# A GpSimd product written in output order, a subtraction moved behind background work, and down blocks with 512 columns

## The chip, the cores and the metric

The kernel runs on one core of a Trainium2 chip. The metric is the device time of one execution in microseconds (us), the lower the better. The core has five engines that run side by side, each with its own in-order queue: PE (TensorE, the matmuls, with the weight loads shown as PEld), DVE (VectorE), ACT (ScalarE), POOL (GpSimd) and SP (SyncE, which here starts the DMAs). They wait for each other through semaphores.

## What is computed

The reference is a block of two attention kinds (MoBA and differential) with an expert layer (PEER), followed by two more attention layers, all in fp32 on 256 tokens of width 1024. The change touches the expert layer alone:

```python
def chunk_fn(xc):                      # tokens of 1024 features
    q = (xc @ w_query).reshape(C, PEER_HEADS, 2, PEER_HALF)
    sc = jnp.einsum('thpd,hpnd->thpn', q, sub_keys)
    top_s, top_i = lax.top_k(sc, PEER_TOPK)
    ...                                # best 16 of the pairs: experts, best_s
    gates = jax.nn.softmax(best_s, axis=-1)
    u = expert_down[experts]
    vv = expert_up[experts]
    act = gelu(jnp.einsum('cd,chkd->chk', xc, u), approximate=False)
    w = gates * act
    return jnp.einsum('chk,chkd->cd', w, vv)
```

There are 16384 experts (128 x 128), 8 heads and 16 chosen experts per head and token.

## The kernel before

**Tiling of the expert layer.** No expert is gathered. The kernel multiplies all tokens with all 16384 down vectors, in 128 blocks of 128 experts, takes the Gelu, multiplies with a dense matrix of gates G (nearly all zero), and multiplies the result with all up vectors, again in 128 blocks. Experts lie on the partitions, the 256 tokens on the free axis. The tile `big` has 100 slots of 128 x 256 for the blocks between down and up; down blocks 100 to 127 use slots 0 to 27 again, so the order (`seq`, in `peer`) is: down 0 to 99, up 0 to 15, down 100 to 115, up 16 to 27, down 116 to 127, up 28 to 127. Blocks go in pairs: `d_pair(j)` makes down blocks j and j+1, `u_pair(j)` up blocks j and j+1.

**fp32 by three products.** Every fp32 operand is split into a hi part (rounded to fp32r) and a lo part (the rest), and `mm3` (L217 to L221) does hi x hi, hi x lo, lo x hi as three matmuls into one PSUM accumulation. Weights arrive as raw fp32 by DMA; `Stream` (L76 to L152) splits each unit of 1024 columns into wh (ACT cast, L119) and wl (DVE subtraction, L129), three units ahead of use. The tokens' parts are nh and nl. A down block is 8 steps of k with three matmuls of 256 columns each. An up block takes the activations as weights: `w_split(j)` makes gh (ACT cast, L892) and gl (DVE subtraction, L893) of a pair's `big` slots one block ahead, and `sum_unit` runs 4 x 3 matmuls of 512 columns.

**Ticks.** G comes in 64 ticks of four tokens for each half of the experts, as background work: `later` queues a step, `run_bg(budget)` after each block runs some two of them. `g_tick` (L913 to L943) makes one-hots o1 and o2 of the two expert indices on DVE (L921, L922), o1h = o1 x gate on GpSimd (L923, written through a rearranged view, so with a step of 64 elements for each new token), and o1l = o1 x lo part of the gate by four ACT activations (L926). Two ticks later `mm` runs the eight small matmuls of the tick (L934, L935) into a bank of PSUM; every second tick DVE multiplies the finished G into `big` (L941). The first half's ticks run beside down blocks 64 to 99, the second half's beside up blocks 28 to 61.

**Queues.** Everything is in program order on each engine. In an up block the order is: `stream.get` (casts of later weights), the 12 matmuls, for the first block of a pair `w_split` of the next pair (gh, then gl), then `run_bg` (the ticks). PSUM has two banks with tag s; a down pair takes one bank for both blocks, and its Gelu (L881) reads the whole bank after the second block.

Of the kernel before, what the change touches and what calls it, by code (L numbers as in the profile page):

```python
# [10 lines left out]
F32R = mybir.dt.float32r  # L11
# [3 lines left out]
AF = mybir.ActivationFunctionType  # L15
ALU = mybir.AluOpType
AX = mybir.AxisListType

P = 128
# [135 lines left out]
class Kernel:  # L155
# [614 lines left out]
    def peer(self, x):  # L770
        tc, nc, A = self.tc, self.nc, self.A
        ident = self.const("ident")
        SLOTS, H = 100, 64
        with (
# [1 line left out]
            tc.tile_pool(name="pew", bufs=3) as pw,  # L776
        ):
            big = pl.tile([P, SLOTS, 256], F32, name="big")
            nh = pl.tile([P, 8, 256], F32R, name="nh")
            nl = pl.tile([P, 8, 256], F32R, name="nl")  # L780
            qT = big[:, 64:80, :]
            sc = big[:, 80:96, :].rearrange("p (t a) b -> p t (a b)", t=2).rearrange("p t (h n) -> p t h n", n=P)
            sk = big[:, 56:64, :].rearrange("p a b -> p (a b)")
# [5 lines left out]
            ghT = pl.tile([P, 256], F16, name="ghT")  # L789
# [16 lines left out]
            TB, GB = 1.5, 1.75  # L806
            with tc.tile_pool(name="peq", bufs=1) as pq:
# [32 lines left out]
                for hp in range(16):  # L840
                    if hp % 2 == 0:
                        qb = self.bank("s")
                    wh, wl = self.stream.get(self.u, hp > 0)
                    o = qb[:, (hp % 2) * 256 : (hp % 2) * 256 + 256]
                    for k in range(8):
                        ks = slice(k * P, k * P + P)
# [20 lines left out]
            with tc.tile_pool(name="pew2", bufs=2) as pw2:  # L867
                def d_pair(j, nxt, budget):
                    hb = self.bank("s")
                    for jj in range(2):  # L870
                        wh, wl = self.stream.get(self.u)
                        if jj == 0 and nxt is not None:
                            w_split(nxt)
                        o = hb[:, jj * 256 : jj * 256 + 256]
                        for k in range(8):
                            ks = slice(k * P, k * P + P)
                            self.mm3(o, wh[:, ks], wl[:, ks], nh[:, k, :], nl[:, k, :], k == 0, k == 7)
                        self.u += 1
                        if jj:
                            sl = j % SLOTS  # L880
                            nc.scalar.activation(  # L881
                                big[:, sl : sl + 2, :].rearrange("p a b -> p (a b)"), hb, AF.Gelu
                            )
                        self.run_bg(budget)

                Ws = {}

                def w_split(j):
                    sl = j % SLOTS
                    wh = pw2.tile([P, 2, 256], F32R, name=self.nm("gh"), tag="gh")  # L890
                    wl = pw2.tile([P, 2, 256], F32R, name=self.nm("gl"), tag="gl")
                    nc.scalar.copy(wh, big[:, sl : sl + 2, :])  # L892
                    nc.vector.tensor_sub(wl, big[:, sl : sl + 2, :], wh)  # L893
                    Ws[j] = (wh, wl)

                def u_pair(j, nxt, budget):
                    if j not in Ws:
                        w_split(j)
                    gh, gl = Ws.pop(j)
                    for jj in range(2):  # L900
                        self.sum_unit(
                            lambda t: (gh[:, jj, t * P : t * P + P], gl[:, jj, t * P : t * P + P]),
                            banks,
                            j + jj == 0,
                            x if j + jj == 127 else None,
                        )
                        if jj == 0 and nxt is not None:
                            w_split(nxt)
                        self.run_bg(budget)

                gp = {}

                def g_tick(half, tb):  # L913
                    def f():
                        tsl = slice(tb * 4, tb * 4 + 4)
                        o2 = pw2.tile([P, P, 4], F16, name=self.nm("o2"), tag="o2", bufs=3)
                        o1 = pw2.tile([P, H, 4], F16, name=self.nm("o1"), tag="o1", bufs=3)
                        o1h = pw2.tile([P, 4, H], F16, name=self.nm("o1h"), tag="o1h", bufs=3)
                        o1l = pw2.tile([P, 4, H], F16, name=self.nm("o1l"), tag="o1l", bufs=3)
                        b = lambda a, n: a[:, tsl].unsqueeze(1).to_broadcast([P, n, 4])  # L920
                        nc.vector.tensor_tensor(o1, iota4[:, half * H : half * H + H, :], b(i1T, H), op=ALU.is_equal)  # L921
                        nc.vector.tensor_tensor(o2, iota4, b(i2T, P), op=ALU.is_equal)  # L922
                        nc.gpsimd.tensor_tensor(o1h.rearrange("p t j -> p j t"), o1, b(ghT, H), op=ALU.mult)  # L923
                        for i in range(4):
                            t = tb * 4 + i
                            nc.scalar.activation(o1l[:, i, :], o1[:, :, i], AF.Copy, scale=glT[:, t : t + 1])  # L926

                        def mm():
                            if tb % 2 == 0:
                                gp[0] = self.bank("t" if tb % 4 == 0 else "o")  # L930
                            g = gp[0]
                            for i in range(4):
                                o = g[:, ((tb % 2) * 4 + i) * H : ((tb % 2) * 4 + i) * H + H]
                                nc.tensor.matmul(o, o2[:, :, i], o1h[:, i, :], start=True, stop=False)  # L934
                                nc.tensor.matmul(o, o2[:, :, i], o1l[:, i, :], start=False, stop=True)  # L935
                            if tb % 2:
                                t8 = slice(tb // 2 * 8, tb // 2 * 8 + 8)
                                gv = g.rearrange("p (t j) -> p j t", t=8)
                                for j0, j1, s0 in ((0, 64, 0),) if half == 0 else ((0, SLOTS - 64, 64), (SLOTS - 64, 64, 0)):
                                    v = big[:, s0 : s0 + j1 - j0, t8]  # L940
                                    nc.vector.scalar_tensor_tensor(v, gv[:, j0:j1, :], 2.0**-14, v, op0=ALU.mult, op1=ALU.mult)  # L941

                        return mm  # L943

                    return f

                def g_ticks(half):
                    pend = []
                    LAG = 2

                    def step(tb):
                        def f():
                            if tb < 64:
                                pend.append(g_tick(half, tb)())
                            if tb >= LAG:
                                pend.pop(0)()

                        return f

                    for tb in range(64 + LAG):  # L960
                        self.later(step(tb), 0, 0.89)

                self.scores(3, qT, sk, sc, rx, top)
                self.later(lambda: self.select(pw, topv, topi, i1T, i2T, ghT, glT, big), 0, 0.5)
                M = 128 - SLOTS
                seq = [("D", j) for j in range(0, SLOTS, 2)]
                for u0, u1 in ((0, 16), (16, M)):
                    seq += [("U", j) for j in range(u0, u1, 2)]
                    seq += [("D", j) for j in range(SLOTS + u0, SLOTS + u1, 2)]
                seq += [("U", j) for j in range(M, 128, 2)]  # L970
                for i, (kind, j) in enumerate(seq):
                    if (kind, j) == ("D", 64):
                        self.flush()
                        g_ticks(0)
                    if (kind, j) in (("D", SLOTS - 2), ("U", 62)):
                        self.flush()
                    if (kind, j) == ("U", 0):
                        banks = [self.bank(f"a{i}") for i in (1, 3, 2, 0)]
                    if (kind, j) == ("U", M):
                        g_ticks(1)  # L980
                    nxt = None
                    if i + 1 < len(seq) and seq[i + 1][0] == "U":
                        nxt = seq[i + 1][1]
                    if kind == "D":
                        d_pair(j, nxt, TB if j < 64 else GB)
                    else:
                        u_pair(j, nxt, GB)

# [771 lines left out]
```

## Time and profile before

| what | value |
|---|---|
| median of 3 runs | 1459.81 us (1459.66 to 1462.8) |
| profiled execution | 1459.06 us |
| its span, first to last instruction | 1457.3 us |
| granted TensorE clock, mean | 0.996 of 2.4 GHz |
| PE busy | 1420.3 us, 97% of the span |
| DVE, ACT, POOL busy | 991.8, 884.2, 409.0 us |

The span is a little shorter than the execution's time, and the profiled execution is 0.75 us below the median of the runs. Matmuls are pipelined: a record of 0.28 us can be followed by the next start 0.12 us later, so the cadence is read from starts, not from durations. DVE and ACT records overlap their successor by some 0.08 us. Blocks stand in time as follows: down 0 to 99 from 197 to 506 us, up 0 to 15 to 549 us, down 100 to 115 to 596 us, up 16 to 27 to 628 us, down 116 to 127 to 663 us, up 28 to 127 to 979 us.

### The profile page before, as it was taken

What the parts mean: (1) busy time and instruction counts of PE and PEld (TensorE: products, weight loads), DVE (VectorE), ACT (ScalarE), POOL (GpSimd) and SP (SyncE); (2) the same over time, 40 slices, a digit from 0 to 9 for tenths busy, and PEclk for the clock granted to TensorE, in tenths of its full rate; (3) what the DMA queues carried; (4) which work ended last, traced back from release to release, by engine and by line L of the source; (5) the groups of instructions that cost most, each with busy time, mean ns of one, the idle gap of its engine ahead of it and who ended that gap; (6) DMA issues with size and microseconds to landing.
All of it is one profiled execution on the core that took longest, in us unless ns stands there. A gap on an engine that the chain in (4) does not pass through costs nothing.

```text
span 1457.3 us, 24829 instructions
## 1 busy us (share of the span) xinstructions
PE 1420.3 (97%) x9375; PEld 1240.1 (85%) x9375; DVE 991.8 (68%) x1985; ACT 884.2 (61%) x1723; POOL 409.0 (28%) x626
## 2 busy tenths in 40 slices
PE   9899999999999999999888999999999999999998
PEld 7677999999999989897666888887888888887887
DVE  6666899997699854548999555556554566665444
ACT  5675554544699844547878454456766667766653
POOL 4760300000377500004666000007232543117200
PEclk9999999999999999999999999999999999999999
DMA  7334445555444455554333555565444554445422
GB/s 252 142 116 150 150 172 190 184 178 182 165 146 148 172 202 175 196 180 144 123 139 118 201 201 198 183 225 172 164 173 157 172 188 157 148 164 194 168 97 87
DMA packets 50935, 243.14 MB, mean 167 GB/s; under 512 B 4224, under 2 KB 11520, under 8 KB 31488
## 3 DMA queue, kind: packets, MB, share of 16 engines
q1 hardware_dynamic: 50528, 241.04, 47.3%
q8 instruction: 73, 1.20, 0.3%
q10 hardware_dynamic: 288, 0.52, 0.1%
q14 instruction: 46, 0.38, 0.1%
HBM read 240.50 MB, written 1.05 MB: 166 GB/s over the span
## 4 chain that ended last, share of the span: by engine, by line
PE 82%; DVE 5%; POOL 5%; ACT 5%; issue 3%; DMA 1%; DVEq 0%; ACTq 0%; POOLq 0%
PE a L219 14%; PE a L221 14%; PE a L220 14%; PE s L219 10%; PE s L220 10%; PE s L221 9%; PE s L1365 2%; DVE big L941 1%; ACT wh L119 1%; ACT o1l L926 1%; DVE o L921 1%; DVE o L922 1%; PE o L1441 1%; PE o L1449 1%; DVE wl L129 1%
## 5 line engine op out<-in xcount | busy, mean ns | idle before, releaser
L129 DVE TENSOR_TENSOR wl<-raw,wh 128x1024 fp32r<-128x1024 f32 (+1 forms) x435 | 565.3, 1308 | 140.3 <-ACT wh L119 140.3
L119 ACT CAST wh<-raw 128x1024 fp32r<-128x1024 f32 (+1 forms) x435 | 452.7, 1043 | 258.4 <-PE a L221 187.5
L923 POOL TENSOR_TENSOR o1h<-o,ghT 128x256 f16<-128x256 f16 x128 | 170.7, 1453 | 468.2 <-DVE o L921 456.0
L219 PE MATMUL s<-nh,wh 128*128 128x256 f32 x1024 | 292.6, 286 | 0.0
L220 PE MATMUL s<-nl,wh 128*128 128x256 f32 x1024 | 289.7, 283 | 0.0
L221 PE MATMUL s<-nh,wl 128*128 128x256 f32 x1024 | 289.6, 283 | 0.0
L219 PE MATMUL a<-wh,gh 128*128 128x512 f32 x512 | 202.7, 396 | 0.0
L221 PE MATMUL a<-wh,gl 128*128 128x512 f32 x512 | 199.7, 390 | 0.0
L220 PE MATMUL a<-wl,gh 128*128 128x512 f32 x512 | 199.2, 389 | 0.0
L219 PEld LDWEIGHTS s<-nh,wh 128*128 128x128 f32 x1024 | 196.5, 192 | 0.1
L220 PEld LDWEIGHTS s<-nl,wh 128*128 128x128 f32 x1024 | 196.5, 192 | 0.1
L221 PEld LDWEIGHTS s<-nh,wl 128*128 128x128 f32 x1024 | 196.3, 192 | 0.0
L926 ACT ACTIVATE o1l<-o,glT 128x64 f16<-128x64 f16 x512 | 138.1, 342 | 32.3 <-DVE o L921 25.7
L219 PE MATMUL a<-wh,xha 128*128 128x512 f32 x320 | 132.4, 414 | 0.5 <-DVE xha L282 0.5
L221 PE MATMUL a<-wh,xla 128*128 128x512 f32 x320 | 125.4, 392 | 0.0
L220 PE MATMUL a<-wl,xha 128*128 128x512 f32 x320 | 125.2, 391 | 0.0
L893 DVE TENSOR_TENSOR gl<-big,gh 128x512 fp32r<-128x512 f32 x64 | 44.3, 692 | 106.9 <-ACT gh L892 106.9
L221 PEld LDWEIGHTS a<-wh,gl 128*128 128x128 f32 x512 | 96.1, 188 | 20.8
L220 PEld LDWEIGHTS a<-wl,gh 128*128 128x128 f32 x512 | 96.3, 188 | 18.9
L219 PEld LDWEIGHTS a<-wh,gh 128*128 128x128 f32 x512 | 96.3, 188 | 18.8
L881 ACT ACTIVATE big<-s 128x512 f32<-128x512 f32 x64 | 38.1, 595 | 91.6 <-PE s L221 91.4
L1370 DVE CUSTOM_DVE_ANT_0 e<-s,bias 128x128 f32<-128x128 f32 (+2 forms) x128 | 34.1, 327 | 71.2 <-PE s L1365 71.2
(409 smaller groups left out, 2499.5 us busy)
## 6 DMA issues: line engine op xcount, KB each, us to landing
raw<-in_peer_down_dram SPq DMA_DIRECT2D x64, 1024.0 KB, 4.8
raw<-in_peer_up_dram SPq DMA_DIRECT2D x64, 1024.0 KB, 4.9
raw<-in_a_w_in_dram SPq DMA_DIRECT2D x40, 1024.0 KB, 4.9
raw<-in_b_w_in_dram SPq DMA_DIRECT2D x16, 1024.0 KB, 4.8
raw<-in_w_in_dram SPq DMA_DIRECT2D x10, 1024.0 KB, 5.0
raw<-in_peer_query_dram SPq DMA_DIRECT2D x8, 1024.0 KB, 4.8
raw<-in_w_out_dram SPq DMA_DIRECT2D x4, 1024.0 KB, 5.0
bias<-in_bias_dram SPq DMA_DIRECT2D x8, 512.0 KB, 5.8
```

What stands on the lines that cost most here:

```text
L119: self.nc.scalar.copy(hi[:, c], self.part(u)[:, c])
L129: eng.tensor_sub(lo[:, c], self.part(u)[:, c], hi[:, c])
L219: nc.tensor.matmul(o, lh, rh, start=start, stop=False)
L220: nc.tensor.matmul(o, lh, rl, start=False, stop=False)
L221: nc.tensor.matmul(o, ll, rh, start=False, stop=stop)
L881: nc.scalar.activation(big[:, sl : sl + 2, :].rearrange("p a b -> p (a b)"), hb, AF.Gelu)
L893: nc.vector.tensor_sub(wl, big[:, sl : sl + 2, :], wh)
L921: nc.vector.tensor_tensor(o1, iota4[:, half * H : half * H + H, :], b(i1T, H), op=ALU.is_equal)
L923: nc.gpsimd.tensor_tensor(o1h.rearrange("p t j -> p j t"), o1, b(ghT, H), op=ALU.mult)
L926: nc.scalar.activation(o1l[:, i, :], o1[:, :, i], AF.Copy, scale=glT[:, t : t + 1])
L1365: nc.tensor.matmul(o, l, r, start=start, stop=stop)
L1370: nc.vector.tensor_tensor_reduce(e[:, c], s[:, c], bts[i][:, qt * w : qt * w + w], -1.0, 3.0e38, ALU.add, ALU.min, nmx[g][:, h, qt : qt + 1],)
```

## The change

Three edits, all in `peer`.

nh and nl become two halves of one tile nhl, so that for each k the 256 columns of nh and the 256 of nl lie side by side. A new `d_dual` takes down pairs 50 to 62 and 100 to 126; in it wh meets both parts in one matmul of 512 columns, wl meets nh in one of 256, each block has a bank of its own, ACT copies the half that came from nl out of PSUM, DVE adds the other half to it, and the Gelu runs once per pair from `big`. `w_split` does its cast at once and returns the subtraction as a function; down pairs call it at once, `u_pair` after `run_bg`. The product o1h is written in the order of its tile, and o1 is read through a rearranged view instead.

```diff
-            nh = pl.tile([P, 8, 256], F32R, name="nh")
-            nl = pl.tile([P, 8, 256], F32R, name="nl")
+            nhl = pl.tile([P, 8, 2, 256], F32R, name="nhl")
+            nh, nl = nhl[:, :, 0, :], nhl[:, :, 1, :]
...
                         if jj == 0 and nxt is not None:
-                            w_split(nxt)
+                            w_split(nxt)()
...
+                def d_dual(j, nxt, budget):
+                    sl = j % SLOTS
+                    for jj in range(2):
+                        hb = self.bank("s")
+                        wh, wl = self.stream.get(self.u)
+                        if jj == 0 and nxt is not None:
+                            w_split(nxt)()
+                        for k in range(8):
+                            ks = slice(k * P, k * P + P)
+                            nc.tensor.matmul(hb, wh[:, ks], nhl[:, k, :, :].rearrange("p a b -> p (a b)"), start=k == 0, stop=False)
+                            nc.tensor.matmul(hb[:, 0:256], wl[:, ks], nh[:, k, :], start=False, stop=k == 7)
+                        self.u += 1
+                        v = big[:, sl + jj, :]
+                        nc.scalar.copy(v, hb[:, 256:512])
+                        nc.vector.tensor_tensor(v, hb[:, 0:256], v, op=ALU.add)
+                        if jj:
+                            v = big[:, sl : sl + 2, :].rearrange("p a b -> p (a b)")
+                            nc.scalar.activation(v, v, AF.Gelu)
+                        self.run_bg(budget)
...
                     nc.scalar.copy(wh, big[:, sl : sl + 2, :])
-                    nc.vector.tensor_sub(wl, big[:, sl : sl + 2, :], wh)
                     Ws[j] = (wh, wl)
+                    return lambda: nc.vector.tensor_sub(wl, big[:, sl : sl + 2, :], wh)
...
-                        if jj == 0 and nxt is not None:
-                            w_split(nxt)
+                        low = w_split(nxt) if jj == 0 and nxt is not None else lambda: None
                         self.run_bg(budget)
+                        low()
...
-                        nc.gpsimd.tensor_tensor(o1h.rearrange("p t j -> p j t"), o1, b(ghT, H), op=ALU.mult)
+                        nc.gpsimd.tensor_tensor(o1h, o1.rearrange("p j t -> p t j"), ghT[:, tsl].unsqueeze(2).to_broadcast([P, 4, H]), op=ALU.mult)
...
                     if kind == "D":
-                        d_pair(j, nxt, TB if j < 64 else GB)
+                        (d_dual if j >= SLOTS or 50 <= j < 64 else d_pair)(j, nxt, TB if j < 64 else GB)
```

## Rows read from the trace of the kernel before

**Rows 1.** The page's first part: busy time (share of the span) and instructions.
```profile
PE 1420.3 (97%) x9375; PEld 1240.1 (85%) x9375; DVE 991.8 (68%) x1985; ACT 884.2 (61%) x1723; POOL 409.0 (28%) x626
```

**Rows 2.** Stretches: length, busy of PE, PEld, DVE, ACT, POOL (instructions), clock, DMA.
```profile
388.00:500.00 112.00, 112.00 (x1276) 110.62 (x1274) 109.05 (x185) 104.68 (x301) 81.56 (x61) 1.00 0.42 146
549.00:595.00 46.00, 46.00 (x383) 45.90 (x382) 20.35 (x18) 20.67 (x24) 0.00 (x0) 1.00 0.51 177
668.50:799.70 131.20, 115.36 (x894) 89.94 (x892) 122.40 (x235) 106.39 (x300) 83.42 (x63) 1.00 0.38 129
```

**Rows 3.** PE's groups, 668.5 to 799.7: busy, mean ns, idle before, releaser.
```profile
L219 PE MATMUL a<-wh,gh 128*128 128x512 f32 x128 | 53.1, 415 | 0.0
...
L934 PE MATMUL t<-o1h,o 128*128 128x64 f16 x127 | 12.9, 199 | 9.7 <-POOL o1h L923 9.7
```

**Rows 4.** The chain in order of time, 709 to 721: start us, us, what.
```profile
711.17 1.07 ACT o1l L926 x4
712.24 0.95 ACT wh L119
713.20 0.53 ACT gh L892
...
713.75 0.04 DVE gl L893
```

**Rows 5.** DVE in order of time, up block ticks: start us, us, instruction, idle before.
```profile
713.75 0.69 DVE L893 TENSOR_TENSOR gl<-big,gh 128x512 fp32r<-128x512 f32 x1 [0.52 <-ACT gh L892]
...
719.29 0.41 DVE L922 TENSOR_TENSOR o<-iota4h,i2T 128x512 f16<-128x512 f16 x1
719.62 1.87 DVE L129 TENSOR_TENSOR wl<-raw,wh 128x1024 fp32r<-128x1024 f32 x1
722.04 0.69 DVE L893 TENSOR_TENSOR gl<-big,gh 128x512 fp32r<-128x512 f32 x1 [0.55 <-ACT gh L892]
```

**Rows 6.** PE in order of time: 256 columns, 512 columns, two tick blocks' starts.
```profile
553.78 0.28 PE L219 MATMUL s<-nh,wh 128*128 128x256 f32 x1
553.90 0.28 PE L220 MATMUL s<-nl,wh 128*128 128x256 f32 x1
...
820.24 0.39 PE L219 MATMUL a<-wh,gh 128*128 128x512 f32 x1
820.46 0.39 PE L220 MATMUL a<-wl,gh 128*128 128x512 f32 x1
...
402.05 0.36 PE L219 MATMUL s<-nh,wh 128*128 128x256 f32 x1
...
405.56 0.36 PE L219 MATMUL s<-nh,wh 128*128 128x256 f32 x1
```

**Rows 7.** DVE in order of time: three casts wl beside fp32 products on GpSimd.
```profile
19.78 1.23 DVE L129 TENSOR_TENSOR wl<-raw,wh 128x1024 fp32r<-128x1024 f32 x1 [2.25 <-ACT wh L119]
...
61.67 1.22 DVE L129 TENSOR_TENSOR wl<-raw,wh 128x1024 fp32r<-128x1024 f32 x1
...
1336.95 1.99 DVE L129 TENSOR_TENSOR wl<-raw,wh 128x1024 fp32r<-128x1024 f32 x1 [1.05 <-ACT wh L119]
```

**Rows 8.** POOL in order of time: fp32 products beside those casts, and one alone.
```profile
19.90 1.44 POOL L480 TENSOR_TENSOR tab_k_moba_s<-consts 128x128 f32<-128x128 f32 x1
...
61.65 1.83 POOL L541 TENSOR_TENSOR mc<-mc,ms 128x256 f32<-128x256 f32 x1 [5.42 <-PE a L221]
63.45 0.73 POOL L542 TENSOR_TENSOR mc<-mc,ms 128x256 f32<-128x256 f32 x1
...
1336.82 1.04 POOL L1257 TENSOR_TENSOR rw<-rw,rk 128x512 f32<-128x512 f32 x1
```

**Rows 9.** POOL in order of time: the second product of an up block.
```profile
719.51 1.47 POOL L923 TENSOR_TENSOR o1h<-o,ghT 128x256 f16<-128x256 f16 x1
```

**Rows 10.** Groups of ACT and DVE that read 256 columns of PSUM.
```profile
L1116 ACT CAST ghT<-o 128x256 f16<-128x256 f32 x1 | 0.4, 372 | 0.1
...
L1119 DVE TENSOR_TENSOR glT<-o,ghT 128x256 f32<-128x256 f32 x1 | 0.4, 423 | 4.0 <-ACT ghT L1116 4.0
```

More of the change, by code (lines that the diff above doesn't have):

```diff
@@ L892, in w_split @@
                     nc.scalar.copy(wh, big[:, sl : sl + 2, :])
-                    nc.vector.tensor_sub(wl, big[:, sl : sl + 2, :], wh)
                     Ws[j] = (wh, wl)
+                    return lambda: nc.vector.tensor_sub(wl, big[:, sl : sl + 2, :], wh)
                 def u_pair(j, nxt, budget):
                     if j not in Ws:
-                        w_split(j)
+                        w_split(j)()
                     gh, gl = Ws.pop(j)
```

## The prediction

> **What bounds the kernel now.** The first part of the page comes first: PE is busy 97% of the span [rows 1], so only what shortens PE's own stream, or a stall of PE, can show. Next the busy time by stage [rows 2] says where PE is not dense. In the two stages of expert blocks shown first (388 to 500 us, the down blocks with the first half's ticks; 549 to 595 us, down blocks without ticks) it is busy all the time; in 668.5 to 799.7 us, the up blocks with the second half's ticks, it is busy 115.36 of 131.2 us. The groups of that stretch [rows 3] give 128 matmuls of L219, four to a block, so 32 blocks or 16 pairs: 8.20 us a pair. They also name what the tick's matmuls of L934 wait for: GpSimd's product o1h (L923).
>
> The page of who waits would stop there and blame GpSimd. The chain of waits of one pair [rows 4] says something else: it goes four activations o1l, then the cast wh, then the cast gh on ACT, then gl on DVE (713.20 to 713.75), and only then DVE's one-hot of the next tick. DVE's order in time [rows 5] shows the same: gl at 713.75 sat 0.52 us idle for gh, and again at 722.04, one pair later. Since the one-hots of the tick stand behind gl in DVE's queue, the product, and with it PE, is late by that wait. So the stage runs around a loop DVE, ACT, DVE; GpSimd only passes the lateness on.
>
> What each engine would need by itself for a pair there: DVE 722.04 - 713.75 = 8.29 us less the wait. gl begins 0.55 us after wl ends (719.62 + 1.87 = 721.49), where an instruction with nothing to wait for begins 0.08 us before its predecessor's end (719.62 against 719.29 + 0.41), so 0.63 us are lost and DVE needs 7.66 us [rows 5]. ACT: four times 1.07 for o1l, two casts wh of 0.95, one gh of 0.53 = 6.7 us [rows 4]. PE: a down block without ticks is 24 steps of 0.12 us = 2.88 us, with two ticks 405.56 - 402.05 = 3.51 us, so two ticks cost 0.63 us; an up block is 12 steps of 0.227 us = 2.72 us; 3.35 us together, 6.7 us a pair [rows 6]. DVE is therefore what ends last once the wait is gone.
>
> **The lo part behind the ticks.** w_split now casts gh at once and u_pair calls the subtraction gl after run_bg. DVE's instructions stay the same in number; gl moves behind the one-hots and the PSUM product of two ticks (L921, L922, L941). What now queues behind it is the next wl, as before. Nothing on DVE waits for gh any more, since gh stands on ACT ahead of the ticks' o1l and is long done. PE needs gl only in the third matmul of the pair after, one whole block later, so the move itself costs nothing; its cover is that block of 3.4 us or more, against some 2.3 us for the ticks and gl. What is gained is at most 8.20 - 7.66 = 0.54 us a pair, 16 x 0.54 = 8.6 us; next late is DVE by its own sum. In up blocks without ticks nothing stands between, so nothing changes there.
>
> **The product in output order.** One GpSimd instruction for one, 128 of them, same 256 elements; it now writes o1h contiguously and reads o1 with a step of four elements. How long it takes in this form no row shows. It matters twice, but not by its own length: the product begins 0.1 us after its one-hot whenever it can, and two of them never fill a block. It matters by what it does to wl. Undisturbed, wl takes 1.22 us (the row at 61.67) [rows 7]; behind a product it takes 1.87 us [rows 5]. The rows of fp32 products show how: when GpSimd starts first, wl ends 1.08 us after GpSimd's end (1336.95 + 1.99 against 1336.82 + 1.04), so it stood still until then; when DVE starts first, the product stretches from 0.73 to 1.83 us and ends 0.59 us after wl (61.65 + 1.83 against 61.67 + 1.22) [rows 7, 8]. They take turns. The fp16 product is odd: it ends at 719.51 + 1.47 = 720.98 [rows 9], yet wl ends at 721.49, only 0.51 us later, so its reading let go 0.57 us before its end. I read that as a read phase followed by a slow tail of writes with a step of 128 bytes.
>
> In output order I take the fp32 product of 256 elements as the nearest row: o2 frees DVE at 719.70, the product ends 0.59 us later at 720.29, wl ends at 721.37 instead of 721.49. That is 0.12 us a block, 0.24 us a pair, DVE's pair is 7.42 us, and the stage gains 16 x (8.20 - 7.42) = 12.5 us together with the part above. Bounds: the fp32 product of 128 elements, the same bytes as 256 of fp16, ends 0.33 us after wl (19.90 + 1.44 against 19.78 + 1.23) [rows 7, 8], which would save 0.38 us a block; and if the strided read held DVE until the product's end as it is now (720.98), wl would end at 722.06, 0.57 us later than now. In the down blocks with ticks (388 to 500 us, 112 / 3.51 = 32 blocks) DVE is busy 109 of 112 us and PE all of it [rows 2]: a shorter hold buys nothing there, since PE's 3.51 us stand, but a longer one costs in full.
>
> The Trainium skill, GPSIMD Engine Reference, section Performance pitfalls for Q7 kernels, says that reads whose step is over 8 bytes cost about half as much again per element; four fp16 elements are 8 bytes, so by it the new read just stays free. If the step counted as over, the hold would be an estimated 0.59 x 1.5 = 0.89 us instead of the 0.71 us now (719.70 to 720.41), and the sum would come to about 1458 us. No run here shows the new read yet.
>
> **Down blocks with both parts as one operand.** d_dual takes pairs 50 to 62 and 100 to 126: 7 + 14 pairs, 42 blocks, 336 steps of k. Each step had three matmuls of 256 columns, 0.12 us apart, 0.36 us; now one of 512 (0.227 us) and one of 256 (0.12 us), 0.347 us [rows 6]. 336 x 0.013 = 4.4 us. Bounds: nothing, if a 512 between 256s costs two of them; twice that, 8.8 us, if the other fixed part is hidden too. I take the middle, because both cadences are rows of the same matmul form.
>
> The Trainium skill, TensorE: Matmul & The Clock Gate, section Back-to-back issue gap, puts the fixed part at 2.5 ns a matmul: one matmul less would save an estimated 336 x 2.5 ns = 0.8 us. The rows here show 13 ns (0.12 us for 256 columns, 0.227 us for 512), so by the trace it is 4.4 us.
>
> Added per block: an ACT copy from PSUM (0.37 us for 256 columns) and a DVE add with one PSUM operand (0.42 us), and the Gelu now reads SBUF [rows 10]. In 549 to 595 us, 16 blocks, DVE is busy 20.4 and ACT 20.7 of 46 us [rows 2]; 16 x 0.42 and 16 x 0.37 fit. New waits: ACT's copy waits for the block's last matmul with the next cast wh behind it, DVE's add waits for the copy with the next wl behind it; both casts are for a block three further on. A bank is used per block instead of per pair, and there are two: the third block needs the first's bank. It is free about 0.1 + 0.37 + 0.1 + 0.42 = 1.0 us after the block's end, and asked for 2.8 us after it. If that cover went, PE would lose the difference in each of 42 blocks.
>
> **Sum.** Profiled execution 1459.06 us (its span is 1457.3): 1459.06 - 4.4 - 12.5 = 1442.2. The median of the runs is 0.75 us above the profiled one, so 1442.9, about **1443 us**.
>
> **The rivals.** (1) The product keeps its time, because fp16 and not the order makes it slow; then the change of order doesn't do what it says. For it: no fp16 product in another order is in the trace. Only gl moving and the dual blocks count: 1459.8 - 4.4 - 8.6 = 1446.8. (2) The port goes by bytes and the hold falls to the 0.33 us of the small fp32 product: DVE's pair is 7.66 - 0.76 = 6.90 us, just above ACT's and PE's 6.7; 16 x 1.30 = 20.8, so 1434.6. (3) The strided read holds DVE longer than the contiguous one did. Each 0.1 us more costs 32 blocks in the down ticks and 32 in the up ticks, 6.4 us; it decides from 13.0 / 64 = 0.20 us on, above which the kernel is slower. If the hold lasts until the present end of the product, 0.57 us more, 1446.8 + 36.5 = 1483. Against it: reading is not what made the tail of 0.57 us. (4) The same with the hold longer by 0.15 to 0.20 us: 1456 to 1460, no change.
>
> **How the numbers follow.** Forecast 0.48, rival (1) 0.24 (with small lengthenings up to 1455), (2) 0.13, (3) 0.10, (4) 0.05. A difference within 0.2%, 2.9 us, can't be told from no change here. The range, 1434 to 1455, takes in (1), (2) and the bounds of the dual blocks, and leaves (3) and (4) out. Faster 0.84, same 0.05, slower 0.11; faster and forecast go the same way, so one range serves.
>
> **What would show it.** Right: no wait of gl for gh in 668 to 800 us; the pair near 7.4 us; wl near 1.75 us in both tick stretches; the product's record near 0.7 to 0.9 us; 0.347 us a step and blocks of 2.77 us from 549 us on; DVE still dense in the up ticks. Wrong: wl above 1.87 us, or down blocks with ticks above 3.51 us (rival 3); the product at 1.45 us (rival 1); PE dense through the up ticks (rival 2); steps of 0.36 us, or PE waiting for a bank after a dual block.

## The result and the profile after

The changed kernel takes **1439.33 us** (median of 4 runs, 1437.36 to 1444.05) against 1460.66 us for the kernel before beside it: a ratio of 0.9859, 95% interval 0.9835 to 0.9883, some 21 us or 1.4% less. The forecast was 1443 us, in a range of 1434 to 1455. Its profiled execution has a span of 1438.0 us (1457.3 before).

Where the time went is read from the starts of the first matmul of each block. The table gives stretches of blocks in us, in the profiled executions; "dual" are the down blocks made by `d_dual`.

| stretch | before | after | difference |
|---|---|---|---|
| down 0 to 49 | 144.07 | 144.07 | 0 |
| down 50 to 63 (dual after) | 40.96 | 40.23 | -0.73 |
| down 65 to 97 (first half's ticks) | 115.25 | 115.17 | -0.08 |
| up 0 to 27, without ticks | 76.22 | 76.25 | 0.03 |
| down 100 to 127 (dual after) | 80.62 | 79.12 | -1.50 |
| up 28 to 61 (second half's ticks) | 136.95 | 118.38 | -18.57 |
| up 62 to 126 | 176.93 | 176.93 | 0 |

The sum of the differences, 20.85 us, is more than that of the spans, 19.3, because the first block began 1.2 us later (198.12 against 196.93 us) and the layers behind take 0.4 us longer. Both move by as much between executions of the runs below, whatever the edit: the first block begins between 196.93 us (e4, which has the tile nhl too) and 198.86, and the time from the last block's start to the end is 479.1 to 484.1 us. Nine tenths of the gain lie in the up blocks with ticks. The last of these ends where up block 62 begins, at 799.71 us before and 780.05 us after, though the stretch began at nearly the same time. PE in order of time, first after, then before:

```profile
661.67 0.40 PE L219 MATMUL a<-wh,gh 128*128 128x512 f32 x1
...
780.05 0.47 PE L219 MATMUL a<-wh,gh 128*128 128x512 f32 x1
```

```profile
799.71 0.47 PE L219 MATMUL a<-wh,gh 128*128 128x512 f32 x1
```

The page's first part and the product's group, of after. Line numbers moved by 20, that of gl by 21: the product is L943, the one-hots L941 and L942, gl L914, gh L912, the tick's matmuls L954 and L955; L895 and L896 are the matmuls of a dual block.

```profile
PE 1416.2 (98%) x9039; PEld 1221.7 (85%) x9039; DVE 990.9 (69%) x2027; ACT 893.4 (62%) x1765; POOL 327.3 (23%) x626
...
L943 POOL TENSOR_TENSOR o1h<-o,ghT 128x256 f16<-128x256 f16 x128 | 86.9, 679 | 530.5 <-DVE o L941 524.5
```

336 matmuls fewer, and 42 instructions more on DVE and on ACT, as the edit says. The product's record fell from 1.47 [rows 9] to 0.68 us.

The stretches of after that answer to those of before [rows 2], and the up ticks as a whole (length, busy time of PE, PEld, DVE, ACT, POOL with their instructions, clock, DMA):

```profile
388.00:500.00 112.00, 112.00 (x1270) 110.58 (x1270) 103.79 (x186) 102.87 (x300) 42.38 (x62) 1.00 0.42 151
549.00:595.00 46.00, 46.00 (x261) 39.83 (x260) 24.66 (x32) 25.74 (x39) 0.00 (x0) 1.00 0.50 180
...
661.70:780.00 118.30, 117.34 (x921) 92.84 (x920) 116.77 (x241) 107.02 (x309) 43.04 (x64) 1.00 0.44 152
```

In the up ticks DVE is now busy 116.77 of 118.3 us. DVE in order of time shows one pair of up blocks (after):

```profile
704.33 0.41 DVE L942 TENSOR_TENSOR o<-iota4h,i2T 128x512 f16<-128x512 f16 x1
704.66 1.64 DVE L129 TENSOR_TENSOR wl<-raw,wh 128x1024 fp32r<-128x1024 f32 x1
...
707.63 0.41 DVE L942 TENSOR_TENSOR o<-iota4h,i2T 128x512 f16<-128x512 f16 x1
707.96 1.10 DVE L914 TENSOR_TENSOR gl<-big,gh 128x512 fp32r<-128x512 f32 x1
708.99 1.21 DVE L129 TENSOR_TENSOR wl<-raw,wh 128x1024 fp32r<-128x1024 f32 x1
...
711.87 1.64 DVE L129 TENSOR_TENSOR wl<-raw,wh 128x1024 fp32r<-128x1024 f32 x1
```

and GpSimd beside it:

```profile
704.54 0.68 POOL L943 TENSOR_TENSOR o1h<-o,ghT 128x256 f16<-128x256 f16 x1 [0.53 <-DVE o L941]
...
707.85 0.67 POOL L943 TENSOR_TENSOR o1h<-o,ghT 128x256 f16<-128x256 f16 x1 [0.53 <-DVE o L941]
```

gl has no idle time before it any more (0.52 us before [rows 5]); it stands behind the one-hots and takes the turn that wl took: stretched from 0.69 to 1.10 us where it follows a product, while the wl behind it is at its undisturbed 1.21 us. From wl to wl the pair is 711.87 - 704.66 = 7.21 us; it was 8.29 [rows 5].

### The profile page after: what moved, and what is told of

Its sections match the earlier page's. It is cut to its first block, busy times and chain, and to the rows that moved or that the text cites. A ratio compares the mean times of both kernels' runs of the same rounds, so it can differ in the third digit from the quotient of the medians.

```text
span 1438.0 us, 24233 instructions
## 1 busy us (share of the span) xinstructions
PE 1416.2 (98%) x9039; PEld 1221.7 (85%) x9039; DVE 990.9 (69%) x2027; ACT 893.4 (62%) x1765; POOL 327.3 (23%) x626
## 4 chain that ended last, share of the span: by engine, by line
PE 85%; DVE 6%; POOL 4%; issue 2%; ACT 2%; DMA 1%; DVEq 0%; POOLq 0%; ACTq 0%
PE a L219 15%; PE a L221 15%; PE a L220 15%; PE s L219 7%; PE s L220 7%; PE s L221 7%; PE s L895 5%; PE s L896 3%; PE s L1385 2%; DVE big L961 1%; DVE o L942 1%; PE o L1461 1%; DVE gl L914 1%; DVE wl L129 1%; PE o L1469 1%
## 5 line engine op out<-in xcount | busy, mean ns | idle before, releaser
L129 DVE TENSOR_TENSOR wl<-raw,wh 128x1024 fp32r<-128x1024 f32 (+1 forms) x435 | 546.0, 1263 | 81.5 <-ACT wh L119 81.4
L943 POOL TENSOR_TENSOR o1h<-o,ghT 128x256 f16<-128x256 f16 x128 | 86.9, 679 | 530.5 <-DVE o L941 524.5
L219 PE MATMUL s<-nhl,wh 128*128 128x256 f32 x688 | 197.4, 287 | 0.0
L220 PE MATMUL s<-nhl,wh 128*128 128x256 f32 x688 | 194.6, 283 | 0.0
L221 PE MATMUL s<-nhl,wl 128*128 128x256 f32 x688 | 194.5, 283 | 0.0
L946 ACT ACTIVATE o1l<-o,glT 128x64 f16<-128x64 f16 x512 | 135.0, 343 | 14.9 <-DVE o L941 13.3
L219 PEld LDWEIGHTS s<-nhl,wh 128*128 128x128 f32 x688 | 131.9, 192 | 0.0
L220 PEld LDWEIGHTS s<-nhl,wh 128*128 128x128 f32 x688 | 132.0, 192 | 0.0
L221 PEld LDWEIGHTS s<-nhl,wl 128*128 128x128 f32 x688 | 131.8, 192 | 0.0
L895 PE MATMUL s<-nhl,wh 128*128 128x512 f32 x336 | 119.0, 399 | 0.0
L219 PEld LDWEIGHTS a<-wh,gh 128*128 128x128 f32 x512 | 96.2, 188 | 19.3
L914 DVE TENSOR_TENSOR gl<-big,gh 128x512 fp32r<-128x512 f32 x64 | 50.1, 782 | 89.1 <-ACT gh L912 89.1
L896 PE MATMUL s<-nhl,wl 128*128 128x256 f32 x336 | 94.4, 281 | 0.0
```

Of the source, the lines that this page charges most:

```text
L129: eng.tensor_sub(lo[:, c], self.part(u)[:, c], hi[:, c])
L219: nc.tensor.matmul(o, lh, rh, start=start, stop=False)
L220: nc.tensor.matmul(o, lh, rl, start=False, stop=False)
L221: nc.tensor.matmul(o, ll, rh, start=False, stop=stop)
L895: nc.tensor.matmul(hb, wh[:, ks], nhl[:, k, :, :].rearrange("p a b -> p (a b)"), start=k == 0, stop=False)
L896: nc.tensor.matmul(hb[:, 0:256], wl[:, ks], nh[:, k, :], start=False, stop=k == 7)
```

## The experiments

The first four take the change apart, the others test what they left. Two theories were against each other for the up ticks. Theory A, the prediction's: a loop from the one-hot over o1l, wh, gh and gl to the next one-hot. Theory B, what a reader of the waits alone would say [rows 3]: PE waits for the product because the product is slow.

### e1: the subtraction behind the ticks, alone

All diffs are against the kernel after. Here the old product and d_pair everywhere come back:

```diff
-    (d_dual if j >= SLOTS or 50 <= j < 64 else d_pair)(j, nxt, TB if j < 64 else GB)
+    d_pair(j, nxt, TB if j < 64 else GB)
-    nc.gpsimd.tensor_tensor(o1h, o1.rearrange("p j t -> p t j"), ghT[:, tsl].unsqueeze(2).to_broadcast([P, 4, H]), op=ALU.mult)
+    nc.gpsimd.tensor_tensor(o1h.rearrange("p t j -> p j t"), o1, b(ghT, H), op=ALU.mult)
```

> Only the subtraction gl moves behind the ticks; the product and the down blocks are as before. Theory A (the up ticks ran around the loop one-hot, o1l, wh, gh, gl, one-hot; GpSimd only passed the lateness on): the wait of gl for gh is gone, DVE's own sum bounds, 7.66 us a pair instead of 8.29, PE runs ahead in the first blocks; up blocks 28 to 61 take about 126 us instead of 136.95, the kernel about 1450 us. Theory B (PE waits for the product because the product takes 1.45 us): nothing changes, 1460 us.

Measured: 1449.68 us, ratio 0.9926 (0.9909 to 0.9942); up blocks 28 to 61 take 126.28 us. DVE in order of time (e1):

```profile
712.82 1.34 DVE L914 TENSOR_TENSOR gl<-big,gh 128x512 fp32r<-128x512 f32 x1
...
716.96 1.88 DVE L129 TENSOR_TENSOR wl<-raw,wh 128x1024 fp32r<-128x1024 f32 x1
...
720.50 1.34 DVE L914 TENSOR_TENSOR gl<-big,gh 128x512 fp32r<-128x512 f32 x1
```

and the product's group (e1, 390 to 800 us):

```profile
L943 POOL TENSOR_TENSOR o1h<-o,ghT 128x256 f16<-128x256 f16 x125 | 167.1, 1457 | 233.7 <-DVE o L941 224.4 <-PE o L955 3.8 <-PE t L955 3.5
```

The pair is 720.50 - 712.82 = 7.68 us, against 7.66 forecast. The wait of gl for gh is gone though the product is as slow as ever (a mean of 1457 ns), so theory B falls for this part.

### e2: the product in output order, alone

```diff
-    low = w_split(nxt) if jj == 0 and nxt is not None else lambda: None
+    if jj == 0 and nxt is not None:
+        w_split(nxt)()
     self.run_bg(budget)
-    low()
-    (d_dual if j >= SLOTS or 50 <= j < 64 else d_pair)(j, nxt, TB if j < 64 else GB)
+    d_pair(j, nxt, TB if j < 64 else GB)
```

> Only the product is written in output order; gl stays ahead of the ticks. Theory A: product near 0.68 us, wl 1.64 instead of 1.87 us, but the loop through gh and gl stays and holds one wl, so a pair takes about 8.05 us, up blocks 28 to 61 about 133 us, the kernel about 1456 us. Theory B: the product's 0.77 us are what PE waited for, twice a pair, so nearly all of the 18.6 us comes back, 1442 us.

Measured: 1456.0 us, ratio 0.9967 (0.9955 to 0.998); up blocks 28 to 61 take 131.74 us. DVE in order of time (e2):

```profile
713.34 0.69 DVE L914 TENSOR_TENSOR gl<-big,gh 128x512 fp32r<-128x512 f32 x1 [0.78 <-ACT gh L912]
...
718.98 1.64 DVE L129 TENSOR_TENSOR wl<-raw,wh 128x1024 fp32r<-128x1024 f32 x1
721.39 0.69 DVE L914 TENSOR_TENSOR gl<-big,gh 128x512 fp32r<-128x512 f32 x1 [0.78 <-ACT gh L912]
```

The product's mean is 676 ns, half of what it was, wl is 1.64 us, and the pair is 721.39 - 713.34 = 8.05 us, as the loop says. What wl gave, DVE now spends waiting: gl sits 0.78 us for gh instead of 0.52. Theory B wanted 1442 us.

### e3: the dual blocks, alone

```diff
-    low = w_split(nxt) if jj == 0 and nxt is not None else lambda: None
+    if jj == 0 and nxt is not None:
+        w_split(nxt)()
     self.run_bg(budget)
-    low()
-    nc.gpsimd.tensor_tensor(o1h, o1.rearrange("p j t -> p t j"), ghT[:, tsl].unsqueeze(2).to_broadcast([P, 4, H]), op=ALU.mult)
+    nc.gpsimd.tensor_tensor(o1h.rearrange("p t j -> p j t"), o1, b(ghT, H), op=ALU.mult)
```

> Only the 42 down blocks with one operand of 512 columns. By the cadences of before, 0.347 us a step, 4.4 us in all, 1456 us. By the trace of after, where a step takes 0.354 us because a 512 behind a 256 takes 0.236 us: 2.2 us, 1458.3 us, and the up ticks as before (137 us).

Measured: 1456.92 us, ratio 0.9977 (0.9968 to 0.9987). The interval, 1.9 to 4.7 us, holds both numbers; the stage times decide: 14 blocks in 40.23 us and 28 in 79.12, 2.23 us less than before, and the same as in after. The up ticks gain nothing from the dual blocks: they take 137.67 us here, 0.7 us more than before. PE in order of time (after):

```profile
559.72 0.40 PE L895 MATMUL s<-nhl,wh 128*128 128x512 f32 x1
559.96 0.28 PE L896 MATMUL s<-nhl,wl 128*128 128x256 f32 x1
560.07 0.40 PE L895 MATMUL s<-nhl,wh 128*128 128x512 f32 x1
```

A step is 0.354 us over a block (2.83 / 8), not 0.347: the 512 takes 0.24 us where the 256 takes 0.11 to 0.12.

### e4: subtraction and product, without the dual blocks

```diff
-    (d_dual if j >= SLOTS or 50 <= j < 64 else d_pair)(j, nxt, TB if j < 64 else GB)
+    d_pair(j, nxt, TB if j < 64 else GB)
```

> Subtraction behind the ticks and product in output order, down blocks as before. Theory A: each helps the other, since without the wait DVE's sum is what a shorter wl shortens; up blocks 28 to 61 about 118.4 us as with all three, the kernel 1441.7 us, so more than the two alone together if these give 11 and 4. If the dual blocks set up the state in which the up ticks start, less.

Measured: 1440.85 us, ratio 0.9867 (0.985 to 0.9883); up blocks 28 to 61 take 118.35 us. Alone the two save 136.95 - 126.28 = 10.67 and 136.95 - 131.74 = 5.21 us there, together 18.60: 2.7 us more than their sum. Once DVE waits for nothing, all of a shorter wl and gl counts; with the wait in the loop about half of it becomes more waiting (e2). The dual blocks are no part of this, since after takes 118.38 us there.

### e5: the 512s of a dual block first, then its 256s

```diff
     nc.tensor.matmul(hb, wh[:, ks], nhl[:, k, :, :].rearrange("p a b -> p (a b)"), start=k == 0, stop=False)
+for k in range(8):
+    ks = slice(k * P, k * P + P)
     nc.tensor.matmul(hb[:, 0:256], wl[:, ks], nh[:, k, :], start=False, stop=k == 7)
```

> As after, but each dual block runs its eight matmuls of 512 columns first and then its eight of 256. Theory A (a 512 takes 0.236 us instead of 0.227 only where it follows a 256): 512s at 0.227 us, a block 2.78 us instead of 2.83, 2 us less in the 42 blocks, 1437 us. Theory B (the 0.236 us belong to any 512 of these blocks, whatever its neighbour): blocks stay at 2.83 us, 1439 us.

Measured: 1438.01 us, ratio 0.9835 (0.9819 to 0.9851). The blocks decide again: 16 in 44.67 us, 2.79 us each, against 45.21 in after; 42 blocks save 1.4 us more. PE in order of time, merged (e5):

```profile
559.98 2.00 PE L895 MATMUL s<-nhl,wh 128*128 128x512 f32 x8
561.82 1.11 PE L898 MATMUL s<-nhl,wl 128*128 128x256 f32 x8
562.78 0.40 PE L895 MATMUL s<-nhl,wh 128*128 128x512 f32 x1
```

Eight 512s start over 561.82 - 559.98 = 1.84 us, 0.230 each; eight 256s over 0.96 us, 0.120 each. A step of k costs 0.349 us so, against 0.354 alternating and 0.347 forecast. So most of what the prediction missed per step is tied to the alternation. Why a 512 next to a 256 takes longer stays open.

### e6: the even ticks' product on VectorE

```diff
-    nc.gpsimd.tensor_tensor(o1h, o1.rearrange("p j t -> p t j"), ghT[:, tsl].unsqueeze(2).to_broadcast([P, 4, H]), op=ALU.mult)
+    (nc.gpsimd if tb % 2 else nc.vector).tensor_tensor(o1h, o1.rearrange("p j t -> p t j"), ghT[:, tsl].unsqueeze(2).to_broadcast([P, 4, H]), op=ALU.mult)
```

> As after, but the products of the even ticks, the second of each up block, run on VectorE. Theory A (wl and gl are stretched only because that product reads just before them): wl back at 1.22 us and gl at 0.69 us, DVE pays about 0.25 us a block for the product, its pair falls from 7.2 to about 6.75 us, PE's 6.83 bound, up blocks 28 to 61 about 116 us, the kernel 1437 us. Theory B (wl is slower there for another reason, such as the DMA or the fp16 one-hots): wl stays at 1.64 us, the pair grows to 7.7 us, the kernel 1444 us.

Measured: 1435.22 us, ratio 0.9819 (0.9803 to 0.9836); up blocks 28 to 61 take 116.11 us. DVE in order of time (e6):

```profile
704.59 0.41 DVE L943 TENSOR_TENSOR o1h<-o,ghT 128x256 f16<-128x256 f16 x1
704.92 1.22 DVE L129 TENSOR_TENSOR wl<-raw,wh 128x1024 fp32r<-128x1024 f32 x1
...
707.80 0.42 DVE L943 TENSOR_TENSOR o1h<-o,ghT 128x256 f16<-128x256 f16 x1
708.13 0.69 DVE L914 TENSOR_TENSOR gl<-big,gh 128x512 fp32r<-128x512 f32 x1
...
711.94 1.22 DVE L129 TENSOR_TENSOR wl<-raw,wh 128x1024 fp32r<-128x1024 f32 x1
```

wl is back at 1.22 us and gl at 0.69, with the one-hots, the DMA and the block as they were. So it is GpSimd's product just ahead that stretches them. My price for the product on DVE was low: it takes 0.33 us from start to start, not 0.25. The pair there is 711.94 - 704.92 = 7.02 us, not 6.75; with 0.25 the sum would have been 7.21 - 0.42 - 0.41 + 2 x 0.25 = 6.88, so the sum was low as well. At 7.02 us DVE is still over PE's own two blocks of 3.41 us, and it still sets the pace in the middle of the stretch: blocks 30 to 41 take 3.41 us, blocks 42 to 56 take 3.59 and 3.42 us in turn. PE in order of time (e6), blocks 43 to 45:

```profile
712.62 0.47 PE L219 MATMUL a<-wh,gh 128*128 128x512 f32 x1
...
716.05 0.47 PE L219 MATMUL a<-wh,gh 128*128 128x512 f32 x1
...
719.64 0.47 PE L219 MATMUL a<-wh,gh 128*128 128x512 f32 x1
```

So PE runs at its own pace only until its lead at the stretch's beginning is spent, and the 116 us forecast were met by another way than the one given.

### e7: the product contiguous on both sides

```diff
-    o1h = pw2.tile([P, 4, H], F16, name=self.nm("o1h"), tag="o1h", bufs=3)
+    o1h = pw2.tile([P, H, 4], F16, name=self.nm("o1h"), tag="o1h", bufs=3)
-    nc.gpsimd.tensor_tensor(o1h, o1.rearrange("p j t -> p t j"), ghT[:, tsl].unsqueeze(2).to_broadcast([P, 4, H]), op=ALU.mult)
+    nc.gpsimd.tensor_tensor(o1h, o1, b(ghT, H), op=ALU.mult)
-    nc.tensor.matmul(o, o2[:, :, i], o1h[:, i, :], start=True, stop=False)
+    nc.tensor.matmul(o, o2[:, :, i], o1h[:, :, i], start=True, stop=False)
```

> As after, but o1h lies in the order of o1, so the product reads and writes without a step, and the tick's matmuls read o1h with a step of four. Theory A (only the strided write made the old product slow): product near 0.68 us and wl at 1.64 us as in after, no change, 1439 us, unless the strided read costs PE something in the ticks. Theory B (the strided read still costs GpSimd time): product below 0.6 us, wl below 1.55 us, DVE's pair below 7.0 us, 1437 us.

Measured: 1448.36 us, ratio 0.9915 (0.9893 to 0.9938). The product's group (e7, 390 to 800 us) and DVE in order of time (e7):

```profile
L943 POOL TENSOR_TENSOR o1h<-o,ghT 128x256 f16<-128x256 f16 x125 | 83.7, 669 | 312.8 <-DVE o L941 306.4 <-DVE o L942 3.4 <-PE t L955 2.4
...
710.37 1.64 DVE L129 TENSOR_TENSOR wl<-raw,wh 128x1024 fp32r<-128x1024 f32 x1
```

The product has a mean of 669 ns (676 in e2) and wl is 1.64 us: reading o1 with a step of four elements costs GpSimd nothing, and writing with a step of 64 elements was the whole difference to 1.45 us. The price goes to PE. Three of the tick's matmuls in order of time (e7):

```profile
443.47 0.22 PE L954 MATMUL o<-o1h,o 128*128 128x64 f16 x1
443.51 0.21 PE L955 MATMUL o<-o1l,o 128*128 128x64 f16 x1
443.56 0.22 PE L954 MATMUL o<-o1h,o 128*128 128x64 f16 x1
```

and three with o1h in the order of before (after):

```profile
670.61 0.20 PE L954 MATMUL o<-o1h,o 128*128 128x64 f16 x1
670.65 0.20 PE L955 MATMUL o<-o1l,o 128*128 128x64 f16 x1
670.68 0.20 PE L954 MATMUL o<-o1h,o 128*128 128x64 f16 x1
```

0.09 us a pair of matmuls instead of 0.07. In the down blocks with ticks, where PE has no slack, 33 blocks go from 115.17 to 120.92 us. The up ticks lose 2.1 us too (118.38 to 120.49), with blocks of some 3.6 us from block 30 on (57 aside), so PE has no lead to spend any more: its own pace there is an estimated 3.41 + 0.17 us, the 0.17 taken from the down blocks ((120.92 - 115.17) / 33). So the layout of o1h that before and after share is worth keeping for PE's sake; it costs a step on GpSimd's side, which is free on the read and was not on the write.

### e8: e5 and e6 together

> e5 and e6 together: the 512s and the 256s of a dual block grouped, the even ticks' product on VectorE. They touch different stages, so if both readings hold the stage times stand side by side: dual blocks at 2.79 us, up blocks 28 to 61 at 116.1 us, about 3.7 us less than after, 1435.5 us or, by the times of e5 and e6, 1434. If one hides the other, no better than e6, 1435.2 us.

Measured: 1434.75 us (1434.42 to 1434.85, 5 runs), ratio 0.9825 (0.9811 to 0.9838). Dual blocks at 2.79 us and up ticks in 116.12 us stand side by side, so each is as it was alone. Its time is the lowest of the runs here, under both kernels; against e6 alone the 0.5 us are less than runs can tell, and the stage times carry the claim.

## Why the prediction was right

**The sum.** The mechanism held, but the number owes something to luck. The up ticks gained 18.57 us instead of 12.5, 6.1 too little forecast; the dual blocks 2.2 instead of 4.4, 2.2 too much; and 1.6 us were lost where no edit stands. For the profiled execution 1442.2 - 6.1 + 2.2 + 1.6 = 1439.9, measured 1439.79: the errors cancel in part.

**The bound.** Right. The wait that PE's groups name was a wait for GpSimd [rows 3], but the chain [rows 4] had it as a loop through gh and gl, and e1 and e2 give the loop's own numbers: 7.68 us for 7.66, and 8.05 us where the loop is left with a shorter wl. Halving the product's time without opening the loop gave 5.2 of 18.6 us.

**The subtraction behind the ticks.** Right in mechanism and pair, low in the sum: 8.6 us forecast, 10.67 measured in e1. The step that failed is "at most 0.54 us a pair": all 32 blocks were put at DVE's pace. PE in order of time (after) shows the stretch's beginning and its middle:

```profile
670.81 0.47 PE L219 MATMUL a<-wh,gh 128*128 128x512 f32 x1
...
674.22 0.47 PE L219 MATMUL a<-wh,gh 128*128 128x512 f32 x1
...
705.66 0.48 PE L219 MATMUL a<-wh,gh 128*128 128x512 f32 x1
...
709.09 0.48 PE L219 MATMUL a<-wh,gh 128*128 128x512 f32 x1
...
712.87 0.48 PE L219 MATMUL a<-wh,gh 128*128 128x512 f32 x1
```

Blocks 30 to 37 take 3.41 to 3.43 us, PE's own pace (the prediction's 3.35 us was 0.06 low). A tick is made two ticks, so one block, before its matmuls use it, and PE can eat that lead first; that the lead comes from there alone is not shown. From block 38 on DVE's pace of 3.6 us shows as blocks of 3.78 and 3.43 us in turn. Toward the end (blocks 57 to 61) it is 3.1 to 3.4 us again. So a slower engine beside PE costs nothing until the lead is spent. For after, these 13 blocks, 30 to 37 and 57 to 61, save 4.2 us against the forecast 3.71 us a block; in e1, where DVE needs 3.84 us a block, the lead is spent by block 34. PE's busy time, 117.34 of 118.3 us, hides the wait, because matmul records overlap; the starts show it.

**The product.** Right in mechanism: it counted through wl and gl and not through its own length, and the forecast of turns held in what it does to wl. wl ends 1.08 us after the product's end (704.66 + 1.64 = 706.30 against 704.54 + 0.68 = 705.22), as the fp32 rows gave it [rows 7, 8]. The mis-sized term is the turn: fp32's 0.59 us behind DVE's last instruction was taken, 0.48 us it is for fp16 (707.85 + 0.67 = 708.52 against 707.63 + 0.41 = 708.04). So wl is 1.64 and not 1.75 us, and the pair 7.21 and not 7.42 us: 2.0 us in the 19 blocks 38 to 56. With the 4.2 us of the lead this makes 18.6 us instead of the 12.5 forecast. The reading of the fp16 row of before [rows 9], a read phase and a tail of strided writes, is borne out: in after and in e7 the writes are contiguous, and the tail is gone with the read's step and without it. One row beside it was read too closely: the prediction puts the fp32 product at 61.65 down as starting after wl, but its record starts 0.02 us before that of wl at 61.67 [rows 7, 8], so the rows do not settle who gets the turn when both start together.

The Trainium skill, SBUF — State Buffer, section SBUF: two separate sides, says that of a VectorE instruction with two SBUF inputs and a GpSimd instruction that reads SBUF the one that starts first keeps the ports they share for the whole instruction, and the other is blocked. The traces agree wherever the product writes contiguously (the 1.08 us above); before the change wl ended only 0.51 us after the product, 0.57 us less, so there the rule gives too long a wait.

**The dual blocks.** Too large: 4.4 us forecast, 2.2 measured. The step that failed is "a 512 takes 0.227 us", taken from a stretch of 512s alone and put behind a 256, where it takes 0.24 us (e3); why is open. The added copy and add cost nothing, as forecast: no wait for a bank, DVE 24.66 and ACT 25.74 of 46 us. e5 shows that grouping the matmuls by width brings 3.6 us. By the fixed part of 2.5 ns that the Trainium skill, TensorE: Matmul & The Clock Gate, section Back-to-back issue gap, gives for an isolated matmul, the estimate was 0.8 us. The measured 2.2 us lie between it and the 4.4 us by the cadences of before.

**The down blocks with ticks.** Right: DVE fell from 109.05 [rows 2] to 103.79 of 112 us there, and the blocks stayed at 3.49 us, PE's own.

**The rivals.** That the product keeps its time is out (0.68 us). That the strided read holds DVE longer, the slower side, is out by e7 (wl is the same with and without the step). Rival 2, a hold of 0.33 us and PE dense at 1434.6, did not come true either: the hold came out between, at 0.48 us, and DVE still sets the pace of blocks 38 to 56. That the time fell below the forecast is the lead's doing for two thirds (4.2 of 6.1 us).

## What to carry to other kernels

A wait that the profile puts on one engine may be the end of a loop: follow the chain through a whole period, add up each engine's own work in it, and break the loop at its idle place first; a faster link in a loop turns in part into more waiting elsewhere (5.2 us alone, 7.9 on top of the broken loop). Where GpSimd and VectorE work side by side, cost a GpSimd instruction by what it does to the next VectorE instruction with two SBUF inputs, and put behind it one that does not need the turn (the ticks' product from PSUM, L961, takes 0.74 us beside GpSimd's old product, in e1, and beside its new one). And price a matmul by the cadence of the sequence that it will stand in, not by that of a pure one.

## What was not expected of the hardware

GpSimd's write order decides the product's time: 1.45 us with a step of 64 fp16 elements on the write side, 0.68 us with a contiguous write, and the read's step of four makes no difference (0.67 us). On PE the step of four is not free: where the operand that streams through the array (o1h) is read with it, a pair of matmuls of 64 columns, one of them so read, takes 0.09 us instead of 0.07. And a 512-column matmul that alternates with 256-column ones takes 0.24 us, against 0.230 among its like in the same blocks (e5).
